# Windowed attention on one core: landing buffers for every load, GpSimd copies to fixed operand addresses, and another order of transfers

## The chip, the cores and the metric

One core of a Trainium2 chip runs the whole program; the other cores are idle. The metric is the device time of one execution in microseconds. Each kernel is timed several times; one execution is also recorded by the hardware profiler (for the changed kernel and the experiments it is one of the timed ones). Engines: PE is TensorE, PEld its weight loads, DVE VectorE, ACT ScalarE, POOL GpSimd, SP SyncE.

## The reference

Softmax attention inside windows of 64 rows, with 4 x 4096 rows of 1536 float32 values in each of q, k, v:

```python
B, S, D = 4, 4096, 1536; W = 64; nw = S // W
logits = np.einsum('bnwd,bnud->bnwu', q_w, k_w) * D ** -0.5   # q_w: (B, nw, W, D)
attn = softmax(logits)                                        # over the last axis
out = np.einsum('bnwu,bnud->bnwd', attn, v_w)                 # float32
```

Each input is read once (302 MB in all), the output written once (101 MB).

## The kernel before

The 16,384 rows are cut into 32 blocks (called units in the code) of 512. In each, TensorE transposes q and k (float16 pairs seen as float32), multiplies them, and after the exponentials multiplies by v. Loads cast float32 to float16 and are issued by GpSimd, as are the stores. TensorE's program is a loop over blocks, so its operands have fixed addresses: `q16`, `k16`, `v16`. VectorE and ScalarE raise `m_q`, `m_k`, `m_v` when TensorE has read the operand for the last time; only then may GpSimd load the next one there. The first blocks and the last v go by way of other buffers (cut). The main loop of GpSimd:

```python
for u in range(1, N - 1):                  # N = 32
    gp.wait_ge(m_q, u + 1)
    load("q", u + 1, q16, d_q)
    # ... (u == 1: v of block 1 copied from its staging place)
    if u + 1 < N - 1:
        store(u - 1)
    gp.wait_ge(m_k, u + 1)
    load("k", u + 1, k16, d_k)
    if u + 1 == N - 1:
        load("v", u + 1, vs, d_vs)
        store(u - 1)
    # ... (u == 1: v of block 2 copied from vs)
    elif u + 1 < N - 1:
        gp.wait_ge(m_v, u + 1)
        load("v", u + 1, v16, d_v)
gp.wait_ge(m_q, N)
store(N - 2)
# ... the last block is stored in two halves, by GpSimd and by SyncE
```

Note the order of transfers, which turns out to matter: **q, store, k, v**.

Of the kernel before, what the change touches and what calls it, by code (L numbers as in the profile page):

```python
# [8 lines left out]
FP16 = mybir.dt.float16  # L9
FP32 = mybir.dt.float32  # L10

P = 128
# [5 lines left out]
def kernel(  # L18
# [4 lines left out]
    v: bass.AP,  # L23
    out: bass.AP,
):



# [2 lines left out]
    nc = tc.nc  # L31
    PE, DVE, ACT = (getattr(mybir.EngineType, e) for e in ("PE", "DVE", "Activation"))
    B, S, D = q.shape
    DC = D // (2 * P)
    NJ = D // 512
    SLOTS, R, H = 4, 2, 2
# [5 lines left out]
    def sb(name, shape, dtype):  # L42
        return ctx.enter_context(nc.sbuf_tensor(name, shape, dtype))
# [6 lines left out]
    def sem(name):  # L50
        sems.append(nc.alloc_semaphore(name))
        return sems[-1]
# [1 line left out]
    q16 = sb("q16", [P, SLOTS, D], FP16)  # L54
    k16 = sb("k16", [P, SLOTS, D], FP16)
    v16 = sb("v16", [P, SLOTS, D], FP16)
    vs = sb("vs", [P, SLOTS, D], FP16)
    xq = sb("xq", [P, DC, UR], FP32)
    xk = sb("xk", [P, DC, UR], FP32)
    NO = 3  # L60
# [8 lines left out]
    ops = [ps(f"o{j}", [P, 512]) for j in range(NJ)]  # L69
    sp = ps("sp", [P, 4])  # L70

    d_r0, d_r1, d_r2, d_q, d_k, d_v, d_vs, d_q1, d_k1, d_v1 = (
        sem(n) for n in ("d_r0", "d_r1", "d_r2", "d_q", "d_k", "d_v", "d_vs", "d_q1", "d_k1", "d_v1")
    )
    d_o = [sem(f"d_o{i}") for i in range(NO)]
    d_l = [sem(f"d_l{i}") for i in range(2)]
    g_q, g_k, g_v = (sem(n) for n in ("g_q", "g_k", "g_v"))
# [8 lines left out]

    m_q, m_k, m_v = (sem(n) for n in ("m_q", "m_k", "m_v"))
    n_e = [sem("n_ed"), sem("n_ea")]
    i_d, i_p, c_q, done = sem("i_d"), sem("i_p"), sem("c_q"), sem("done")

    def on_act(n, j):
        return (n + j) % 2 == 0
# [3 lines left out]

    def slots(t, lo, hi, r):
        return t[:, lo:hi, :].rearrange("p (h r) d -> p h (r d)", r=r)

    def staged(i, half):  # L100

        return outs[i][:, 2 * half : 2 * half + 2, :].bitcast(FP16).rearrange(
            "p a (b d) -> p (a b) d", d=D
        )

    def load(name, u, dst, s):
        src = {"q": qf, "k": kf, "v": vf}[name]
        r = R if name == "v" else SLOTS
        nc.gpsimd.dma_start(  # L109
            out=slots(dst, 0, SLOTS, r), in_=rows(src, u * UR, SLOTS, r)  # L110
        ).then_inc(s, 16)
# [123 lines left out]
    def vector_unit(u):  # L235
        ve = nc.vector
        for g in range(0, 2 * DC, 2):
            copy_out(ve, ve.tensor_copy, g)
        if u == N - 1:
            ve.wait_ge(d_vs, 32)  # L240
            ve.wait_ge(m_v, N - 1)
            ve.tensor_copy(out=v16[:, :, :], in_=vs[:, :, :]).then_inc(g_v, 1)
        for n in range(H * R):
            if n % R == 0:
                await_(ve, p_s)
                ve.reciprocal(out=rs[:, n : n + R], in_=sp[:, n : n + R]).then_inc(n_d, 1)  # L246
                await_(ve, n_d)
                ve.sem_inc(n_r, 1)
            if n == 0:
                await_(ve, fr[0])  # L250
            for j in range(NJ):
                if not on_act(n, j):
                    await_(ve, p_o[0])
                    if (n, j) == (H * R - 1, NJ - 1):
                        ve.sem_inc(m_v, 1)  # L255
                    ins = ve.tensor_scalar_mul(  # L256
                        scaled(u, n, j), bank(n, j), scalar1=rs[:, n : n + 1]
                    )
                    told(ins, u, n, j, 0)
# [25 lines left out]
    def store(u):  # L285
        nc.gpsimd.dma_start(
            out=rows(of, u * UR, SLOTS, R), in_=slots(outs[u % NO], 0, SLOTS, R)
        ).then_inc(d_o[u % NO], 16)

    def unstage(src, dst, s):  # L290

        nc.gpsimd.tensor_copy(
            out=dst[:, :, :].bitcast(FP32), in_=src[:, :, :].bitcast(FP32)
        ).then_inc(s, 1)

    with tc.tile_critical(no_gpsimd_drain=True):

        raw = rows(qf, 0, SLOTS, SLOTS).rearrange("p h (r d) -> p (h r) d", d=D)
        for sl, s in ((slice(0, 1), d_r0), (slice(1, 2), d_r1), (slice(2, SLOTS), d_r2)):
            nc.sync.dma_start(out=outs[0][:, sl, :], in_=raw[:, sl, :]).then_inc(s, 16)  # L300
        nc.vector.memset(ident[:, :], 0.0).then_inc(i_d, 1)
        nc.gpsimd.wait_ge(i_d, 1)
        nc.gpsimd.wait_ge(d_r0, 16)
        nc.gpsimd.affine_select(
            out=ident[:, :], in_=ident[:, :], compare_op=mybir.AluOpType.not_equal,
            fill=1.0, base=0, pattern=[[-1, P]], channel_multiplier=1,
        ).then_inc(i_p, 1)
        load("k", 0, k16, d_k)
        load("v", 0, v16, d_v)

        for i in range(SLOTS):
            nc.gpsimd.wait_ge((d_r0, d_r1, d_r2, d_r2)[i], 16)
            nc.gpsimd.tensor_copy(out=q16[:, i, :], in_=outs[0][:, i, :]).then_inc(c_q, 1)
            if i == 1:
                load("q", 1, staged(2, 0), d_q1)
        load("k", 1, staged(2, 1), d_k1)
        load("v", 1, staged(1, 0), d_v1)
        load("v", 2, vs, d_vs)

        nc.vector.memset(ones[:, :], 1.0).then_inc(i_d, 1)  # L320
        nc.vector.memset(zeros[:, :], 0.0).then_inc(i_d, 1)
        for et in ets:
            nc.vector.memset(et[:, :, :, :], 0.0).then_inc(i_d, 1)
        nc.scalar.wait_ge(i_d, 5)
        nc.scalar.activation(zeros[:, 3:4], zeros[:, 0:1], EXP, bias=zeros[:, 0:1], scale=1.0)

        with nc.Fori(0, N, engines=OrderedEngineSet([PE]), head_slot={PE: 0}):
            tensor_unit()
        assert N % NO == 2
        for eng, unit in ((DVE, vector_unit), (ACT, scalar_unit)):  # L330
            with nc.Fori(0, N // NO, engines=OrderedEngineSet([eng]), head_slot={eng: 0}):
                for u in range(NO):
                    unit(u)
            for u in range(N - 2, N):
                unit(u)

        sy = nc.sync
        for j in range(NJ):
            for n in (2, 3):
                sy.sem_inc(f_o[j][n], 1)  # L340
        for a in range(2):
            sy.sem_inc(fr[a], NO)
        sy.wait_ge(i_p, 1)
        sy.wait_ge(i_d, 5)
        sy.wait_ge(c_q, SLOTS)
        sy.sem_inc(g_q, 1)
        for u in range(N):
            if u >= NO:
                sy.wait_ge(d_o[u % NO], 16 * (u // NO))
                for a in range(2):  # L350
                    sy.sem_inc(fr[a], 1)

            for d, g, n in (
                (d_q, g_q, u - 1 if u > 1 else 0),
                (d_k, g_k, max(u, 1) if u != 1 else 0),
                (d_v, g_v, 1 if u == 0 else u - 1 if 2 < u < N - 1 else 0),
            ):
                if n:
                    sy.sem_inc(g, 1)._wait_ge(d, 16 * n)

        gp = nc.gpsimd
        gp.wait_ge(d_q1, 16)
        gp.wait_ge(m_q, 1)
        unstage(staged(2, 0), q16, g_q)
        gp.wait_ge(d_k1, 16)
        gp.wait_ge(m_k, 1)
        unstage(staged(2, 1), k16, g_k)
        for u in range(1, N - 1):
            gp.wait_ge(m_q, u + 1)
            load("q", u + 1, q16, d_q)  # L370
            if u == 1:
                gp.wait_ge(d_v1, 16)
                gp.wait_ge(m_v, 1)
                unstage(staged(1, 0), v16, g_v)
            if u + 1 < N - 1:
                store(u - 1)
            gp.wait_ge(m_k, u + 1)
            load("k", u + 1, k16, d_k)
            if u + 1 == N - 1:
                load("v", u + 1, vs, d_vs)  # L380
                store(u - 1)
            if u == 1:
                gp.wait_ge(d_vs, 16)
                gp.wait_ge(m_v, 2)
                unstage(vs, v16, g_v)
            elif u + 1 < N - 1:
                gp.wait_ge(m_v, u + 1)
                load("v", u + 1, v16, d_v)
        gp.wait_ge(m_q, N)
        store(N - 2)  # L390


        base, o = (N - 1) * UR, outs[(N - 1) % NO]
        for h, (eng, c) in enumerate(((gp, 1), (sy, 3))):
            for a in range(2):
                eng.wait_ge(n_e[a], c)
            eng.dma_start(
                out=rows(of, base + R * P * h, R, R), in_=slots(o, R * h, R * h + R, R)
            ).then_inc(d_l[h], 16)
        gp.drain()  # L400
        for i in range(NO):
            last = max(u for u in range(N - 1) if u % NO == i)
            sy.wait_ge(d_o[i], 16 * (last // NO + 1))
        for i in range(2):
            sy.wait_ge(d_l[i], 16)
        sy.sem_inc(done, 1)
        gp.wait_ge(done, 1)
        lo, hi = min(s.num for s in sems), max(s.num for s in sems)
        assert hi - lo + 1 == len(sems)
        gp.sem_clear(range(lo, hi + 1))  # L410
# [30 lines left out]
```

## Time and profile before

| | before |
|---|---|
| median of the first 3 runs | 951.55 us (950.38 to 953.58) |
| profiled span | 949.5 us |
| HBM bytes | 402.65 MB, 424 GB/s over the span |
| PE, ACT, POOL busy | 64%, 35%, 10% |

The DMA side is full almost everywhere and no engine is; the prediction below shows the lines and reads them.

### The profile page before, as it was taken

How to read it: one execution, taken by the hardware profiler on the slowest of the kernel's cores; microseconds unless marked ns; L12 is line 12 of the kernel's file. 1: busy time of each engine (PE TensorE's matmuls, PEld its weight loads, DVE VectorE, ACT ScalarE, POOL GpSimd, SP SyncE). 2: the span in 40 equal slices, each digit the busy share in tenths (PEclk: the TensorE clock that was granted, in tenths of full speed). 3: DMA queues.
4: the chain of work that ended last, by engine and by line, in shares of the span. 5: the costliest groups of instructions: out<-in, count | busy, mean ns of one | idle time of the engine just before them, and what ended most of it. 6: DMA issues, size and time to landing. Idle time of an engine off the chain costs nothing. (4 is left out here: it accounts for less than half of the span.)

```text
span 949.5 us, 11240 instructions
## 1 busy us (share of the span) xinstructions
PE 609.7 (64%) x4096; PEld 393.6 (41%) x3456; DVE 278.7 (29%) x454; ACT 331.3 (35%) x642; POOL 97.4 (10%) x140
## 2 busy tenths in 40 slices
PE   2776855577565776656865558655577565776682
PEld 2544543354433444424544335443344433444450
DVE  1331413332133331333322333223332132331341
ACT  1442513443233432234432344323443233432252
POOL 4230100110001100101001010010110001100010
PEclk9997977997788987889887898787997788987796
DMA  9999999999999999999999999999999999999997
GB/s 249 216 284 283 238 247 282 279 284 267 235 277 281 285 280 238 261 280 283 283 254 245 281 280 284 272 234 272 281 283 281 243 256 281 282 282 261 235 236 300
DMA packets 26938, 253.34 MB, mean 267 GB/s; under 512 B 2096, under 2 KB 2096, under 8 KB 10544
## 3 DMA queue, kind: packets, MB, share of 16 engines
q0 software_dynamic: 26352, 248.52, 99.8%
q1 hardware_dynamic: 576, 4.72, 1.3%
q14 instruction: 8, 0.07, 0.0%
q8 instruction: 2, 0.03, 0.0%
HBM read 301.99 MB, written 100.66 MB: 424 GB/s over the span
## 5 line engine op out<-in xcount | busy, mean ns | idle before, releaser
L148 PE MATMUL tp<-ident,k 128*128 128x128 f32 x768 | 155.1, 349 | 231.4 <-PEq L214 224.9
L148 PEld LDWEIGHTS tp<-ident,k 128*128 128x128 f32 x768 | 120.4, 182 | 252.1 <-issue 249.6
L160 PE MATMUL lt<-xq,xk 128*128 128x256 f16 x1536 | 216.1, 293 | 0.0
L223 ACT COPY xk<-tp 128x512 f32<-128x512 f32 x96 | 59.2, 617 | 417.8 <-ACTq L214 417.8
L223 DVE COPY xk<-tp 128x512 f32<-128x512 f32 x96 | 66.5, 692 | 381.8 <-DVEq L214 381.8
L160 PEld LDWEIGHTS lt<-xq,xk 128*128 128x128 f16 x1536 | 160.1, 104 | 33.2
L148 PE MATMUL tp<-ident,q 128*128 128x128 f32 x768 | 104.0, 280 | 66.6 <-DVE xq L223 47.1
L148 PEld LDWEIGHTS tp<-ident,q 128*128 128x128 f32 x768 | 86.4, 143 | 100.5 <-issue 99.9
L269 ACT ACTIVATE et<-lt,zeros 32x128 f16<-32x128 f32 x256 | 92.0, 360 | 39.4 <-ACTq L214 36.2
L223 ACT COPY xq<-tp 128x512 f32<-128x512 f32 x96 | 59.3, 617 | 107.3 <-ACTq L214 107.3
L116 PE MATMUL o<-v,et 128*128 128x512 f16 x384 | 93.3, 379 | 0.0
L189 PEld LDWEIGHTS <-et 128*128 128x128 f16 x384 | 30.2, 97 | 151.3 <-issue 114.3
L256 DVE TENSOR_SCALAR out<-o,rs 128x512 f32<-128x512 f32 x128 | 90.2, 747 | 7.7
L223 DVE COPY xq<-tp 128x512 f32<-128x512 f32 x96 | 66.1, 689 | 78.0 <-DVEq L214 78.0
L116 PE MATMUL tp<-v,et 128*128 128x512 f16 x256 | 75.8, 377 | 0.0
L109 POOL DMA_DIRECT2D k<-in_k_dram x31 | 17.4, 562 | 416.5 <-ACTq L221 416.3
L246 DVE RECIPROCAL rs<-sp 128x2 f32<-128x2 f32 x64 | 10.6, 166 | 157.8 <-DVEq L214 157.6
L280 ACT ACTIVATE out<-tp,rs 128x512 f32<-128x512 f32 x64 | 44.0, 688 | 35.8 <-ACTq L214 31.3
L256 DVE TENSOR_SCALAR out<-tp,rs 128x512 f32<-128x512 f32 x64 | 48.1, 751 | 26.2 <-DVEq L214 26.2
L116 PE MATMUL lt<-v,et 128*128 128x512 f16 x128 | 48.3, 377 | 0.0
L109 POOL DMA_DIRECT2D v<-in_v_dram x29 | 20.5, 706 | 238.2 <-DVEq L255 238.2
L280 ACT ACTIVATE out<-o,rs 128x512 f32<-128x512 f32 x64 | 44.1, 688 | 0.0
(26 smaller groups left out, 132.6 us busy)
## 6 DMA issues: line engine op xcount, KB each, us to landing
out_dram<-out POOLq DMA_DIRECT2D x31, 3072.0 KB, 28.5
k<-in_k_dram POOLq DMA_DIRECT2D x31, 1536.0 KB, 20.6
q<-in_q_dram POOLq DMA_DIRECT2D x30, 1536.0 KB, 21.6
v<-in_v_dram POOLq DMA_DIRECT2D x29, 1536.0 KB, 18.9
vs<-in_v_dram POOLq DMA_DIRECT2D x2, 1536.0 KB, 29.7
out<-in_q_dram SPq DMA_DIRECT2D x2, 768.0 KB, 6.5
out<-in_q_dram SPq DMA_DIRECT2D x1, 1536.0 KB, 11.5
out<-in_q_dram POOLq DMA_DIRECT2D x1, 1536.0 KB, 22.7
```

Of the source, the lines that this page charges most:

```text
L109: nc.gpsimd.dma_start(out=slots(dst, 0, SLOTS, r), in_=rows(src, u * UR, SLOTS, r)).then_inc(s, 16)
L116: return nc.tensor.add_instruction(mybir.InstMatmult(name=nc.get_next_instruction_name(), engine=PE, ins=[low(rhs), low(w)], outs=[low(o)] ...
L148: ins = nc.tensor.transpose(tps[g % 2][:, r, j, :], pairs[:, c * P : (c + 1) * P], ident[:, :])
L160: ins = nc.tensor.matmul(lts[h][:, r, :, :], lhsT=halves(xk, c)[:, r, h, :, w], rhs=halves(xq, c)[:, :, h, :, w], start=(c == 0 and w == 0 ...
L189: ld = nc.tensor.ldweights(w)
L223: copy(out=dst, in_=tps[g % 2][:, :, :, :]).then_inc(f_c[g % 4], 1)
L246: ve.reciprocal(out=rs[:, n : n + R], in_=sp[:, n : n + R]).then_inc(n_d, 1)
L256: ins = ve.tensor_scalar_mul(scaled(u, n, j), bank(n, j), scalar1=rs[:, n : n + 1])
L269: ins = sc.activation(ets[h][s, :, :, s], lts[h][s, :, :, s], EXP, bias=zeros[s, 0:1], scale=scale)
L280: ins = sc.activation(scaled(u, n, j), bank(n, j), COPY, bias=0.0, scale=rs[:, n : n + 1])
```

## The change

The intent: GpSimd issues the next load as soon as it has copied a landed one away, instead of when TensorE has consumed it, so that transfers are queued well ahead; and at the end the last loads go ahead of stores that nobody waits for. The core of the diff (first blocks, SyncE's part and the removed VectorE copy of the last v are cut):

```diff
-    vs = sb("vs", [P, SLOTS, D], FP16)
+    ql = sb("ql", [P, SLOTS, D], FP16)
+    kl = sb("kl", [P, SLOTS, D], FP16)
+    NV = 2
+    vls = [sb(f"vl{i}", [P, SLOTS, D], FP16) for i in range(NV)]
...
+    def hand_over(src, dst, d, u, m, g):
+        gp = nc.gpsimd
+        gp.wait_ge(d, 16 * u)
+        gp.wait_ge(m, copies[0] // 3 + 1)
+        gp.tensor_copy(
             out=dst[:, :, :].bitcast(FP32), in_=src[:, :, :].bitcast(FP32)
-        ).then_inc(s, 1)
+        ).then_inc(c_l, 1)
+        copies[0] += 1
+        gp.wait_ge(c_l, copies[0])
+        gp.sem_inc(g, 1)
...
+        for u in range(1, N):
+            hand_over(ql, q16, d_q, u, m_q, g_q)
+            if u + 1 < N:
+                load("q", u + 1, ql, d_q)
+            hand_over(kl, k16, d_k, u, m_k, g_k)
+            if u + 1 < N:
+                load("k", u + 1, kl, d_k)
+            for what in {N - 3: "", N - 2: "-v"}.get(u, "s"):
+                if what == "v":
+                    load("v", N - 1, vls[(N - 1) % NV], d_v[(N - 1) % NV])
+                else:
+                    gp.wait_ge(m_q, u + 1)
+                    store(u - 2 if what == "-" else u - 1)
+            if u == N - 2:
+                store(u - 1)
+            hand_over(vls[u % NV], v16, d_v[u % NV], (u + u % NV) // NV, m_v, g_v)
+            if u + NV < N - 1:
+                load("v", u + NV, vls[u % NV], d_v[u % NV])
```

One thing that the few words about the change don't say: the store now follows the load of k. The order is **q, k, store, v**.

> **What bounds the kernel now.** I read the engine shares first, then the DMA row and the queues, then the waits, then windows of the start and the end. On the page:
>
> ```profile
> span 949.5 us, 11240 instructions
> PE 609.7 (64%) x4096; PEld 393.6 (41%) x3456; DVE 278.7 (29%) x454; ACT 331.3 (35%) x642; POOL 97.4 (10%) x140
> DMA  9999999999999999999999999999999999999997
> q0 software_dynamic: 26352, 248.52, 99.8%
> HBM read 301.99 MB, written 100.66 MB: 424 GB/s over the span
> ```
>
> No compute engine is near full; the DMA row is full in every slice but the last. The queue's byte count (253 MB) is smaller than the HBM traffic (402.65 MB) because a load reads float32 and lands float16. So in every GB/s figure of the profile a loading stretch shows half of what HBM gives.
>
> The waits of the kernel before, longest first for TensorE, and the sync engine's own:
>
> ```profile
> PE tp L148 <- PEq L214: 244.1, 33, 16.7
> PE tp L148 <- DVE xq L223: 47.9, 64, 1.0
> SPq L359 <- DMA k<-in_k_dram: 436.9, 31, 15.3
> SPq L359 <- DMA q<-in_q_dram: 243.5, 30, 36.4
> ```
>
> TensorE stands 244 us in 33 places, about one per block of 512 rows (32 blocks). SyncE, which passes on the landings of k, waits on the DMA of k. So TensorE starves for k some 7.5 us in each block. It looks like missing prefetch, but one asks first whether the DMA could have brought k sooner. The load of q for block 5 is issued at 121.48 us and that for block 31 at 886.21 us: (886.21 - 121.48) / 26 = 29.41 us a block. A block moves 3 loads and 1 store of 3.146 MB on the HBM side each, 12.58 MB: 427.9 GB/s, or 7.35 us a transfer. Now the stretches by window (columns: window and length; busy us of PE, PEld, DVE, ACT, POOL; TensorE clock, DMA share, GB/s):
>
> ```profile
> 0.00:40.00 40.00, 20.81 (x136) 13.70 (x116) 10.06 (x20) 12.50 (x23) 12.77 (x16) 1.00 0.97 236
> 100.00:880.00 780.00, 510.76 (x3432) 330.23 (x2893) 229.46 (x373) 275.07 (x535) 67.64 (x107) 0.85 1.02 270
> 880.00:900.00 20.00, 10.54 (x60) 7.87 (x56) 5.53 (x8) 4.91 (x8) 1.26 (x2) 0.74 1.03 225
> 900.00:909.00 9.00, 8.24 (x66) 4.85 (x52) 2.33 (x5) 5.23 (x13) 1.95 (x3) 1.00 0.84 160
> 909.00:943.00 34.00, 19.45 (x140) 10.92 (x111) 13.33 (x21) 12.32 (x24) 1.28 (x2) 0.87 0.99 341
> 943.00:949.50 6.50, 0.00 (x0) 0.00 (x0) 0.00 (x0) 0.00 (x0) 0.00 (x0) 0.50 0.02 9
> ```
>
> From 100 to 880 us the share is 1.02, that is, full. Windows of 3 us near the end with loads alone show 213 to 218 GB/s landed (426 to 436 read), and with stores alone 416 to 438. So loads, stores and the mean of a block all run at one rate, near 428 GB/s. It is a bound of bytes, not of latency. There is just **one hole**, at 900 to 909 us (0.84), and a quiet end of some 7 us after the last data, in which the last completion comes and the program closes.
>
> **What the Trainium skill says.** "DMA: Bandwidth & Descriptors", section Specifications, gives a fabric ceiling of 435 GB/s and an HBM limit of about 358 GB/s a core. The trace's 427.9 is 98% of the first and above the second, so here the first is the one to hold against, and at most 2% of rate is left. The same page, "Issuing engines are not separate DMA queues", says that all issuers share the same 16 engines: more buffers or earlier issues add no rate. The flat 428 GB/s over loads and stores agrees. "SBUF — State Buffer", section "SBUF: two separate sides", says that compute and DMA use separate ports, but that GpSimd and some two-port VectorE instructions lock each other out, and that a blocked GpSimd can't write descriptors. The trace before has GpSimd copies beside other work: during the copy at 34.55 to 37.29 us VectorE's multiply took 0.75 us, its mean over the run, and the DMA in 36 to 39 us landed 217 GB/s, full rate for loads. So no cost of such locks is seen. "GPSIMD Engine Reference", "Elementwise — side-by-side cycle accounting", has a port-bound body of 1.03 cycles an element: 3072 x 1.03 / 1.2 GHz = 2.64 us, an estimate; the trace has 2.75 us, which I use.
>
> **The change, part by part.**
>
> *Copies added.* Four such copies become 93 (31 blocks x q, k, v), so 89 more: 89 x 2.75 = 245 us of GpSimd. The cost of a copy and of an issue:
>
> ```profile
> L292 POOL COPY k<-out 128x3072 f32<-128x3072 f32 x1 | 2.8, 2752 | 4.5 <-DMA out<-in_k_dram 4.5
> L109 POOL DMA_DIRECT2D k<-in_k_dram x31 | 17.4, 562 | 416.5 <-ACTq L221 416.3
> L109 POOL DMA_DIRECT2D v<-in_v_dram x29 | 20.5, 706 | 238.2 <-DVEq L255 238.2
> ```
>
> A block then costs GpSimd 3 x 2.75 + 2 x 0.56 + 2 x 0.71 = 10.8 us of 29.4: no bound. POOL busy should come to about 97 + 245 = 342 us (36%). On the path of one operand a copy adds about 3 us after landing, with its semaphores.
>
> *Loads earlier.* The load of q is now issued when its landing buffer is copied out, not when TensorE has consumed the fixed one. Walk one block, with T = landing of q: q is copied and the next q issued at about T+4; k lands at T+7.35, is copied and reissued by T+12; the store follows, then the copy and reissue of v by T+17. Behind T the queue still holds k, store and v, 22 us of work. So at every issue 10 to 20 us are queued: never empty. But in the kernel before it wasn't empty either, from 100 to 880 us, so this is worth **0 us there**. TensorE needs about 16.9 us from the start of k to the end of a block (864.20 to 881.1) and 5 for q: 22 of 29.4, so it goes on waiting some 7 us, mostly for q instead of k (k is ready only some 7 us after q, so a short wait of 1 to 3 us stays there).
>
> *End.* In the kernel before, q of the last block is issued at 886.21, k not until 902.65, because it waits for TensorE to release k16, and the store that used to lie between them is held back. The queue runs dry at about 901. Now the loads of q and k of the last two blocks follow on the copies, with landings queued ahead of them; stores 28, 29 and 30 come after. The order of the queue becomes q30 k30 q31 k31 s28 v31 s29 s30 s31, each issued before the one ahead is finished by my walk. Hole by share: 9 x (1 - 0.84/1.02) = 1.6 us; by bytes against 215 GB/s: 9 x (1 - 160/215) = 2.3 us. I take **-2.0 us**.
>
> *What the end can give back.* Without the hole the DMA ends at about 942.5 - 2.0 = 940.5, its last transfer (s31) from 933.2. Backwards, 7.35 us each: s30 from 925.8, s29 918.5, v31 911.1, s28 903.8, k31 896.4, q31 889.1. So k30 lands at 889.1, is handed over by 894, TensorE ends block 30 at 911 and block 31 some 20.5 us later, at 931.5: its first half-store goes at about 932, ahead of 933.2. It fits by only 1 us, so I add **+0.3 us** for a slip. The VectorE copy of the last v (1.76 us, 923.8 to 925.6) goes away; TensorE was waiting for the exponentials until 926.2, and stores filled the queue: 0 us.
>
> Sum: 951.55 - 2.0 + 0.3 = 949.85, say **949.8 us**.
>
> **Rivals.** (1) *Prefetch frees TensorE*: the 244 us of waits shrink and the time with them. For it: the large wait. Against it: the DMA share of 1.02 at 98% of the stated ceiling; 402.65 MB at 435 GB/s are 925.6 us, an estimate with the skill's figure, and with 2 us of start and 7 of end 935, a gain of 1.7% at the very most. (2) *GpSimd becomes the bound or starves the queue*: it issues in order, so a wait for m_q ahead of a store holds up v behind it, and a copy delays an issue by 2.75 us. With 10 us queued at the worst it is hidden; were 1 us a block lost after all, it would be +31 us, 982. (3) *The end gets worse*: the last v waits for a copy and the three held stores bunch up; if TensorE finished block 31 some 4 us late, the last store would be alone, +3 us, 953. (4) *The transfers run at another rate*, because more of them are queued or GpSimd uses SBUF at the same time; 0.3% either way is 3 us. The start (loads alone, four queued, GpSimd copying) ran at full rate, so I give it little.
>
> **Range and chances.** The runs of the kernel before spread over 3.2 us themselves; the end can give or take 2 to 3, the rate 2 to 3. Range **946 to 954**. A gain over 2% needs below 932.5, under what (1) leaves at the ceiling: **0.01**. A loss over 2% needs case (2): **0.03**. Within 2%: **0.96**.
>
> **What would show it.** DMA share about 1.02 from 100 us to the end, the dip at 900 to 909 gone; about 29.4 us a block; POOL busy near 340 us; copies at 2.75 us; TensorE's waits for operands still near 240 us in total, now mostly before q; last data near 940 us. The prediction is wrong if the share sinks in the middle, if copies take much over 2.75 us or VectorE's rows grow, or if a block falls clearly below 29.4 us, which would mean that the rate wasn't a ceiling.

## The result, and the profile after

The changed kernel took **947.72 us** (946.70 to 948.15, 4 runs), the kernel before on the same chip 951.33 us (4 runs). The ratio is 0.9957 (95% interval 0.9938 to 0.9977): within 2%, and a real gain of some 4 us. Ratios here are the mean time of one kernel's fast runs over that of the other's of the same rounds, so not quite the ratio of the medians quoted. All runs of all kernels below were in the fast state.

The page of the changed kernel, its head lines:

```profile
span 946.4 us, 11421 instructions
PE 651.0 (69%) x4096; PEld 419.8 (44%) x3456; DVE 279.7 (30%) x453; ACT 332.8 (35%) x642; POOL 341.5 (36%) x229
DMA  9999999999999999999999999999999999999997
q0 software_dynamic: 26352, 248.52, 100.0%
HBM read 301.99 MB, written 100.66 MB: 425 GB/s over the span
```

POOL went from 97.4 to 341.5 us busy, and nothing on the DMA rows shows a difference. The copies in the groups of the page (columns: line, engine, operation, tiles, shape, count; busy us, mean ns; idle before and what ended it), then the waits of TensorE and GpSimd (total us, times, longest):

```profile
L292 POOL COPY q<-ql 128x3072 f32<-128x3072 f32 x31 | 85.0, 2743 | 395.7 <-DMA ql<-in_q_dram 395.5
L292 POOL COPY k<-kl 128x3072 f32<-128x3072 f32 x31 | 85.3, 2751 | 110.5 <-DMA kl<-in_k_dram 110.5
```

```profile
POOL q L292 <- DMA ql<-in_q_dram: 395.5, 30, 16.5
PE tp L147 <- PEq L213: 227.2, 60, 16.4
```

A copy takes 2.74 to 2.75 us, as foretold. TensorE waits about as long as before (227 against 244 us), now in 60 places instead of 33, mostly for q; and GpSimd itself waits 396 us for q to land. So everybody waits for the DMA, as before. Now the windows (columns as in the prediction):

```profile
100.00:880.00 780.00, 551.63 (x3440) 355.88 (x2900) 234.11 (x376) 278.75 (x539) 285.70 (x185) 0.84 1.02 270
880.00:900.00 20.00, 12.55 (x88) 10.59 (x89) 4.16 (x6) 3.77 (x6) 13.39 (x9) 0.83 0.98 193
900.00:909.00 9.00, 7.77 (x51) 2.55 (x28) 4.88 (x9) 6.95 (x15) 3.43 (x2) 1.00 0.99 326
```

The hole at 900 to 909 us is gone (share 0.99, before 0.84), but the 20 us ahead of it now are at 0.98 and 193 GB/s, where the kernel before had 1.03 and 225: there is a new, shallower hole. And a block takes (881.80 - 121.85) / 26 = 29.23 us, from the starts of the copies of q for blocks 4 and 30, against the 29.41 us of the prediction. The two are not measured alike: 29.41 us is taken between issues that wait for TensorE, and between the landings of q for the same blocks the kernel before takes 29.31 us (table below). Even so the gain may have come from where I had put 0 us, the middle.

**A view that the page doesn't print.** Every transfer raises its semaphore 16 times; the Trainium skill ("DMA: Bandwidth & Descriptors", "Why a DMA increments its semaphore by 16 and not by 1") says that the 16 engines finish independently and that each posts one of them. The trace keeps the time of each increment, and its numbers agree: 16 increments for every transfer, over 1.2 us and more in these two traces. The first increment tells how far the fastest engine is, the last one when the data may be used. I worked out from these records, for the 17th, 57th and 121st transfer (about blocks 4, 14 and 30) and for the very last increment (us from the span's start; "spread" is last minus first; these transfers are loads of q in the kernel before and of v in the changed one, and their neighbours of the other kinds show nearly the same spread):

| | 17th: first / last | 57th: first / last | 121st: first / last | spread at the 121st | last of all |
|---|---|---|---|---|---|
| before | 114.27 / 116.44 | 405.92 / 408.48 | 872.56 / 878.46 | 5.90 | 946.09 |
| changed | 112.98 / 114.52 | 404.93 / 407.83 | 871.57 / 874.47 | 2.90 | 942.87 |

In the kernel before **one of the 16 engines falls behind**: at the 121st transfer 15 engines are done within 2.56 us of the first and the last one comes at 5.90 us. From the 57th to the 121st transfer, 16 blocks, the spread grows from 2.56 to 5.90 us, 0.21 us a block. In the changed kernel it stays at 2.90. So over these 16 blocks the fastest engine takes 29.17 us a block in both kernels, and the slowest 29.37 us before and 29.17 us now. The fastest engines gain 1.3 us by block 4 and nothing more (1.0 us at block 30). That gain is another thing than the lag: in the kernel before, the 16th and 17th transfer come 8.11 and 7.61 us after the one ahead by first increments, where some 7.3 is usual, probably because v was issued only at 96.34 us, 2.2 us before the fastest engine was done with what was queued (98.55); no run tests that by itself. By the last increment, which is what anybody waits for, the changed kernel is 4.0 us ahead at the 121st transfer and 3.2 us ahead at the end. So the end, where the prediction had put the whole gain, gave 0.8 us back.

### The profile page after: what moved, and what is told of

It reads as the page before. It is cut to its first block, busy times and chain, and to the rows that moved or that the text cites. A ratio compares the mean times of both kernels' runs of the same rounds, so it can differ in the third digit from the quotient of the medians.

```text
span 946.4 us, 11421 instructions
## 1 busy us (share of the span) xinstructions
PE 651.0 (69%) x4096; PEld 419.8 (44%) x3456; DVE 279.7 (30%) x453; ACT 332.8 (35%) x642; POOL 341.5 (36%) x229
## 5 line engine op out<-in xcount | busy, mean ns | idle before, releaser
L147 PE MATMUL tp<-ident,q 128*128 128x128 f32 x768 | 165.0, 384 | 185.6 <-PEq L213 172.7
L147 PEld LDWEIGHTS tp<-ident,q 128*128 128x128 f32 x768 | 131.2, 200 | 239.4 <-issue 236.8
L292 POOL COPY q<-ql 128x3072 f32<-128x3072 f32 x31 | 85.0, 2743 | 395.7 <-DMA ql<-in_q_dram 395.5
L159 PE MATMUL lt<-xq,xk 128*128 128x256 f16 x1536 | 210.2, 288 | 0.0
L147 PE MATMUL tp<-ident,k 128*128 128x128 f32 x768 | 136.3, 317 | 67.3 <-PEq L213 54.5
L159 PEld LDWEIGHTS lt<-xq,xk 128*128 128x128 f16 x1536 | 156.8, 102 | 30.4
L147 PEld LDWEIGHTS tp<-ident,k 128*128 128x128 f32 x768 | 105.1, 163 | 86.3 <-issue 83.9
L292 POOL COPY k<-kl 128x3072 f32<-128x3072 f32 x31 | 85.3, 2751 | 110.5 <-DMA kl<-in_k_dram 110.5
L292 POOL COPY v<-vl 128x3072 f32<-128x3072 f32 x31 | 85.5, 2758 | 10.4 <-DMA vl<-in_v_dram 10.4
```

Of the source, the lines that this page charges most:

```text
L147: ins = nc.tensor.transpose(tps[g % 2][:, r, j, :], pairs[:, c * P : (c + 1) * P], ident[:, :])
L159: ins = nc.tensor.matmul(lts[h][:, r, :, :], lhsT=halves(xk, c)[:, r, h, :, w], rhs=halves(xq, c)[:, :, h, :, w], start=(c == 0 and w == 0 ...
L292: gp.tensor_copy(out=dst[:, :, :].bitcast(FP32), in_=src[:, :, :].bitcast(FP32)).then_inc(c_l, 1)
```

## The experiments

Two theories were on record. **E** (the prediction's): the gain is the filled hole of the end. **L** (laggard): the gain is the lagging engine, whatever makes it lag. Twelve runs were made in three sessions, each session on one chip and beside the kernel before (medians 952.23, 951.58 and 952.24 us). Experiments 1, 2, 3 and the plain end of 8 are of the first session, 4, 5 and 7 of the second, the rest of the third. All gave correct results but the two pure streams, which are wrong on purpose.

### 1. The changed kernel once more

No edit.

> The changed kernel once more, as a control on this chip. Both theories: ratio 0.996 to the kernel before (about -3.5 us). Theory E (the end: the gain is the filled hole at 900 us) expects nothing of the middle. Theory L (laggard: one of the 16 DMA engines falls behind in the kernel before by some 0.18 us a block, its completion comes 5.9 us after the first at block 30, and only some 0.06 us a block, 2.9 us, in the changed one) expects the spread of the 16 completions to be about 3 us again at block 30; if it is anything else here the laggard is chance.

Measured: 948.3 us, ratio 0.9952 (0.9929 to 0.9975); spread 3.38 us at the 121st transfer. The result holds in another session, and the small spread isn't chance.

### 2. The kernel before with its hole filled

```diff
-            if u + 1 < N - 1:
-                store(u - 1)
+            store(u - 1)
             gp.wait_ge(m_k, u + 1)
             load("k", u + 1, k16, d_k)
             if u + 1 == N - 1:
                 load("v", u + 1, vs, d_vs)
-                store(u - 1)
```

> The kernel before, with store 29 in its usual place ahead of the last load of k, so that the queue has 7.3 us of work while that load waits for TensorE. Theory E: the hole at 900 to 909 us goes and with it 1.6 to 2.3 us (about 949.3). Theory L: the laggard was never idle in that hole (its completions go on every 7.28 us through it), so the dip goes from the DMA share but the time moves by less than 0.7 us.

Measured: 952.29 us, ratio 0.9994 (0.9977 to 1.0011), spread 6.45. The hole is gone and the time isn't less. The windows of this experiment from 900 us on, in two answers of the same view, tell why:

```profile
900.00:909.00 9.00, 8.25 (x66) 4.50 (x49) 2.73 (x5) 5.37 (x12) 1.27 (x2) 1.00 0.99 369
930.00:951.40 21.40, 10.10 (x73) 4.70 (x51) 6.92 (x10) 7.23 (x15) 0.55 (x1) 0.80 0.42 175
```

The dip moved: share 0.99 at 900 us, but 0.42 after 930 us, with TensorE still 10 us busy there. The kernel before has 0.64 from 930 us to its end, with TensorE nearly done:

```profile
930.00:949.50 19.50, 1.75 (x9) 0.20 (x2) 2.43 (x5) 1.84 (x3) 0.57 (x1) 0.60 0.64 272
```

The store put ahead of k delays the last k (landed 922.87 us, before 915.11), so the last block is computed late; its first half-store is issued at 941.03 instead of 931.89 us, when the stores ahead of it are already done (937.84). So this run doesn't refute that the hole cost something; it shows that filling it with a store is no gain, since the last block then comes late. By its time it can't decide between E and L. The increments of the kernel before say more: from q to k of the last block the first increment takes 10.35 us (901.71 to 912.07), the last one 7.28 (907.83 to 915.11). In that hole the fast engines stood idle and the slowest did not, as L had it.

### 3. The kernel before with the other order, and nothing else

```diff
-            if u + 1 < N - 1:
-                store(u - 1)
             gp.wait_ge(m_k, u + 1)
             load("k", u + 1, k16, d_k)
+            if u + 1 < N - 1:
+                store(u - 1)
```

> The kernel before, with each store issued after the load of k instead of before it, the order of transfers (q, k, store, v) that the changed kernel has; no copies, no landing buffers. If the order is what makes the laggard: spread at block 30 falls from 5.9 to about 3 us and the time by 2 to 3 us. If it is the copies or buffers: spread stays near 6 us and the time within 1 us of before.

Measured: **945.9 us**, ratio 0.9930 (0.9911 to 0.9947), spread 3.36. Two moved lines, without a buffer or a copy, gain more than the whole change, and twice what was expected. It ran once more in the third session:

> The kernel before with stores after the load of k, once more, beside the others of this chip: ratio to the kernel before 0.993, about 945.5, if the first result holds; spread about 3.4 us at block 30.

Measured: 945.23 us, ratio 0.9928 (0.9911 to 0.9944), spread 2.98. In the trace of the first of these two runs, the gain on the kernel before by last increments is 1.9 us at the 17th transfer, 3.7 us at the 121st and 5.1 us at the end. Its middle by windows, under that of the kernel before in the prediction, shows that the DMA share can't tell the two apart:

```profile
100.00:880.00 780.00, 556.55 (x3400) 333.49 (x2858) 232.60 (x374) 278.93 (x537) 66.69 (x107) 0.84 1.02 268
```

1.02 here and 1.02 there: a mean over 16 engines says full whether or not one of them lags.

### 4. The changed kernel with the old order

```diff
             if u + 1 < N:
                 load("q", u + 1, ql, d_q)
+            if u < N - 3:
+                gp.wait_ge(m_q, u + 1)
+                store(u - 1)
             hand_over(kl, k16, d_k, u, m_k, g_k)
```

(and the store after the load of k taken out for those blocks)

> The changed kernel with each store (except at its end) issued ahead of the copy of k, so that the order of transfers is q, store, k, v as in the kernel before. Order as cause: spread grows to about 6 us at block 30 and the time by 2 to 3 us, to about 950. Copies or buffers as cause: within 0.7 us of the changed kernel.

Measured: 951.56 us, ratio 1.0002 (0.9983 to 1.0022), spread 5.83. With the order undone, the buffers, the copies and the new end together gain nothing.

### 5. The order of transfers without any compute

The same loads and stores, two buffers each, no TensorE, VectorE or ScalarE work but a memset, no copies; two kernels that differ in the order alone.

> Wrong result on purpose: the same loads and stores, order q, k, store, v, two buffers each, no compute and no GpSimd copies; stores write zeros. The floor of the transfers: 402.65 MB at 428 to 431 GB/s are 934 to 941 us and with start and end about 942 to 949 us. If it comes to 945 or more, the changed kernel is at the floor; if under 940, compute or GpSimd still costs. Theory L with the copies as cause: spread at block 30 like or above the kernel before, near 6 us. With the order as cause: near 3 us or less.

> The same stream in the order q, store, k, v of the kernel before. If the order makes the laggard: spread at block 30 some 3 us more than in the stream of the other order and 2 to 3 us slower. If not: the two streams agree within 0.7 us.

Measured: 948.71 us (ratio 0.9968, 0.9951 to 0.9985) for q, k, store, v; 949.57 us (0.9972, 0.9951 to 0.9993) for q, store, k, v. Spreads at the 121st transfer 3.40 and 5.33, with one engine last in the old order (the 15th increment comes 1.46 us after the first). So the old order has a lagging engine even here, but not the expected 2 to 3 us of time: 0.9 us between the medians, and the intervals overlap. The four runs of the old order fall into two pairs, about 948.4 and 950.7 us, and the one profiled is of the longer pair; whether the lag is there in the shorter one isn't known. And it grows slowly: from the 57th to the 121st transfer the spread gains 0.98 us (0.52 in the new order), with compute 3.3 and more. These streams are no floor either: by bytes they are 1.2 us behind experiment 3 at the start (first increment of their 15th transfer at 114.23 and 114.28 us, of its 17th at 113.00; q of block 0 is one transfer here and three there), they issue the last stores only when the last v has landed (934.38 us in the new order), and kernels with compute beat them.

### 6. What follows the store

```diff
             if u + NV < N - 1:
                 load("v", u + NV, vls[u % NV], d_v[u % NV])
+            if u < N - 3:
+                gp.wait_ge(m_q, u + 1)
+                store(u - 1)
```

(and the store after the load of k taken out for those blocks: order q, k, v, store)

> The changed kernel with each store (but for its end) after the load of v, in the order q, k, v, store, q. It asks what makes the lagging engine: in the order q, store, k, v the store is followed by a load of 12,288-byte packets (k); in q, k, store, v by one of 6,144-byte packets (v). Here it is followed by q, of 12,288-byte packets. If the packets of the next load matter: spread of completions at block 30 near 6 us and about 951. If what matters is that k comes right after q, without a store between them, or anything else: spread near 3 us and 947 to 949.

Measured: 949.95 us, ratio 0.9980 (0.9959 to 1.0001), spread 4.81. With the same end, the new order had 0.9952 and a spread of 3.38 (experiment 1), the old one 1.0002 and 5.83 (experiment 4): this is between them in time, though its interval overlaps both. The spread of 4.81 isn't the lag of the old order: it was 4.51 at the 57th transfer already and grew by 0.30 us since, and five engines, not one, are over 3.3 us behind the first. From the 57th to the 121st transfer the three kernels with compute in the order q, store, k, v grow by 3.34, 3.57 and 3.50 us; all seven with compute in the order q, k, store, v by 0.00 to 0.28. So here, too, no engine keeps falling behind. The packet records were the next thing to look at. A store consists of packets of 12,288 bytes that mostly take 0.46 us. I counted those between 450 and 850 us that took over 0.488 us:

| order, kernel | over 0.488 us | spread at the 121st |
|---|---|---|
| q, store, k, v: before / experiment 2 / 4 | 31 / 29 / 47 | 5.90 / 6.45 / 5.83 |
| q, k, v, store: experiment 6 | 32 | 4.81 |
| q, k, store, v: changed / 1 / 3 / 3 again | 9 / 7 / 5 / 0 | 2.90 / 3.38 / 3.36 / 2.98 |
| the two streams (new / old order) | 0 / 0 | 3.40 / 5.33 |

Where the store is followed by a load of k or q (packets of 12,288 bytes) there are some 30 long packets or more; where v follows (packets of 6,144 bytes) under 10. But the stream in the old order lags without any, and experiment 6 has 32 without a growing lag. Nor are they long enough: in the kernel before the 31 packets exceed 0.46 us by 1.1 us in all, while the spread grew by some 2.9 in these 400 us (an estimate, at 0.21 us a block). So what makes the engine lag is **not settled**: the order decides it, that is shown; by what mechanism, and why one engine, is not. The trace here doesn't number the engines. The Trainium skill ("DMA: Bandwidth & Descriptors", "Latency and other measured facts") says that two of them, 7 and 15, are usually slower and guesses at the fetching of descriptors for GpSimd's transfers; here one engine lags and only in one order, which that alone doesn't explain, and no run shows the cause.

### 7. The cost of the copies

Every copy done twice:

```diff
-        gp.tensor_copy(...).then_inc(c_l, 1)
-        copies[0] += 1
+        for _ in range(2):
+            gp.tensor_copy(...).then_inc(c_l, 1)
+            copies[0] += 1
+            gp.wait_ge(c_l, copies[0])
```

> The changed kernel with every GpSimd copy done twice: POOL busy about 341 + 256 = 597 us. If the copies are hidden behind queued transfers, as predicted, the middle stays at 29.2 us a block and the time grows by under 1 us there, plus up to 3 us at the end where the queue runs low. If GpSimd delays issues on the path: 2.75 us times some of 31 blocks, tens of us.

Measured: 950.15 us, ratio 0.9983 (0.9961 to 1.0005), spread 2.28. From its page, then from its windows:

```profile
PE 657.1 (69%) x4096; PEld 420.7 (44%) x3456; DVE 279.7 (29%) x453; ACT 333.5 (35%) x642; POOL 596.7 (63%) x322
```

```profile
100.00:880.00 780.00, 554.59 (x3446) 356.94 (x2909) 233.09 (x375) 278.14 (x537) 505.24 (x265) 0.84 1.02 270
```

255 us more of GpSimd cost the middle nothing: the 121st transfer is done at 873.73 us, against 874.47 in the changed kernel. The 2 to 3 us that the time grew lie after it, at the end, where the queue is shallow. So the copies are hidden, as predicted.

### 8. The end by itself

The changed kernel with plain stores, each after the load of k, to the end:

```diff
-            for what in {N - 3: "", N - 2: "-v"}.get(u, "s"):
-                ... (as in the diff above)
-            if u == N - 2:
-                store(u - 1)
+            gp.wait_ge(m_q, u + 1)
+            store(u - 1)
```

(and v of the last block loaded as every other)

> The changed kernel without its order of the end: every store right after the load of k, the last v loaded in its usual place. Theory E, as predicted, holds that the reordered end is what gains: without it, 1.5 to 2 us slower than the changed kernel. Rival: the reordered end makes its own dips (share 0.87 at 885 to 888 and under 1 at 894 to 900 us), so without it the dips go and the time is the same or up to 1.5 us faster than the changed kernel (946 to 948).

Measured: 950.54 us, ratio 0.9981 (0.9965 to 0.9998), against 0.9952 of the changed kernel in the same session: by these ratios 2.8 us slower, by medians 2.2 (the intervals overlap a little). So against a plain end the reordered one seems to gain, as E says: with plain stores, store 30 is done at 932.90 us and the first half-store of the last block is issued only at 937.23. The kernel before, however, didn't have a plain end; it had its own early loads. So the changed kernel with the end of the kernel before:

```diff
+            if u == N - 2:
+                load("v", N - 1, vls[(N - 1) % NV], d_v[(N - 1) % NV])
+            gp.wait_ge(m_q, u + 1)
+            store(u - 1)
```

(in place of the same lines)

> The changed kernel with the end of the kernel before: store 28 in its usual place after the load of k, then q31, k31, v31, store 29, store 30. The kernel before in the other order (b_ksv) was 2.4 us faster than the changed kernel on one chip, and both had the same 29.2 us a block and the same time at block 30. If the difference is the changed end, whose held-back stores let the queue run low at 885 to 900 us: about 946, 2 to 3 us faster than the changed kernel. If it is the copies: no gain, 948 or more.

Measured: **944.5 us**, ratio 0.9919 (0.9902 to 0.9935), spread 2.64: the fastest kernel of all, and 3.4 us (0.0036 of 951) better than the changed one by ratios to the kernel before, though of different sessions. What its end has over the changed one is seen in the windows of 3 us. The changed kernel:

```profile
885.00:888.00 3.00, 2.87 (x13) 2.46 (x14) 0.69 (x1) 0.62 (x1) 0.53 (x1) 0.50 0.87 156
...
894.00:897.00 3.00, 3.00 (x29) 2.73 (x28) 0.69 (x1) 0.63 (x1) 3.00 (x3) 1.00 0.95 152
897.00:900.00 3.00, 3.00 (x29) 2.62 (x28) 0.69 (x1) 0.63 (x1) 2.77 (x2) 1.00 0.93 187
```

and this experiment:

```profile
885.00:888.00 3.00, 2.87 (x13) 2.45 (x13) 0.69 (x1) 0.62 (x1) 0.56 (x1) 0.50 0.97 291
...
894.00:897.00 3.00, 3.00 (x20) 2.50 (x21) 0.69 (x1) 0.60 (x2) 3.00 (x2) 0.69 1.04 250
897.00:900.00 3.00, 3.00 (x29) 2.70 (x27) 0.69 (x1) 0.86 (x2) 0.06 (x1) 1.00 1.03 220
```

Loads alone land some 215 GB/s when the queue is full; the changed kernel shows 156, 152 and 187 there. GpSimd's timeline in the changed kernel (start us, length us, operation, idle before) has the cause:

```profile
881.80 2.75 POOL L292 COPY q<-ql 128x3072 f32<-128x3072 f32 x1 [15.18 <-DMA ql<-in_q_dram]
885.13 0.53 POOL L108 DMA_DIRECT2D ql<-in_q_dram  x1 [0.58 <-POOL q L292]
889.07 2.75 POOL L292 COPY k<-kl 128x3072 f32<-128x3072 f32 x1 [3.41 <-DMA kl<-in_k_dram]
892.41 0.53 POOL L108 DMA_DIRECT2D kl<-in_k_dram  x1 [0.58 <-POOL k L292]
892.93 0.71 POOL L281 DMA_DIRECT2D out_dram<-out  x1
```

At 885.13 only the k of block 30 is still under way, and its first engine is done at 886.08: the store that used to be queued behind it is held back. The new q is issued 0.95 us ahead of that, and its first completion comes 8.52 us after the one before instead of 7.3; the following k takes 9.98 us by last increments. Leaving store 28 at its place fills exactly this gap.

Not all of the 3.4 us is this gap as such. In the two traces store 30 is done 3.3 us earlier with the old end (933.17 against 936.47), the last increment only 1.2 us earlier (941.63 against 942.87); the other 2.2 us lie between it and the end of the program, 1.3 against 3.5 us. In all kernels with compute the program ends either about 1.3 us after the last increment of SyncE's half of the last store or about 3.5 us (3.4 to 3.6) after that of GpSimd's, whichever is later; in this experiment it is SyncE's, in the kernel before and the changed one GpSimd's. Whether that follows from the gap isn't tested.

### 9. Stores from SyncE

The changed kernel with a plain end, and its stores 0 to 30 issued by SyncE on a queue of its own.

> The changed kernel with the stores issued by SyncE, on its own queue, so that they share the engines with the loads instead of waiting behind them; GpSimd issues loads alone. By bytes the time stays within 3 us of the changed kernel (loads and stores all run at one rate). If the laggard comes from stores in GpSimd's queue, the spread falls under 2.5 us and the time by 1 to 2 us; if the mixing of two queues costs rate, it is slower.

Measured: 962.55 us, ratio 1.0109 (1.0092 to 1.0126), spread 4.54. The main expectation, a time within 3 us, failed; its last branch, slower, came: against the plain end of experiment 8 (0.9981) it is 1.3% slower. The 121st transfer is done at 881.17 us instead of 873.91, so the loss is there in the middle, with a DMA share of 1.02 again; the mean store packet takes 0.4715 us instead of 0.4611. Stores from SyncE cost rate here. Whether it is the second queue, the place of the stores among the loads or SyncE's own waits (it issues a store and waits for another in turn) isn't separated.

## Why the prediction was right or wrong

The time fell in the range, on the right side and within 2%. The sum came near for reasons that were half wrong: -1.7 us was foretold and some -4 measured, and that it is not further off is luck, since two errors of about 7 and 5 us (the order, the end) were of opposite sign.

- **The bound: right.** Bytes at 16 engines' rate. (Loads alone landed 205 to 227 GB/s in those windows, not 213 to 218; their mean is the 215 that was used.) All kernels with GpSimd stores lie within 1% of each other; doubling GpSimd's work or putting TensorE's waits elsewhere moved nothing in the middle. Rival 1 was dismissed rightly.
- **The copies: right.** 2.75 us each, POOL 341.5 us against 342 predicted, hidden. With the old end they cost nothing measurable (0.9919 with, 0.9928 without, same session).
- **"So this is worth 0 us there": wrong, and the largest error.** I had written the new order of the queue down without noticing that the place of the store in it was a change, and read the mean share of 1.02 as "nothing to gain". Order alone is worth 0.70 to 0.72%, 6.7 to 6.9 us of 952 (experiment 3). By last increments 1.9 us of it come by block 4, about as much again by block 30, and the rest at the end. Of the 1.9 us some 1.1, by first increments, are the late transfers near 100 us, so "just one hole" was wrong too. From block 4 on it is the engine that no longer lags; in my terms rival 4, "another rate", which I had given little. Even the "quiet end of some 7 us after the last data" hid it: six packets of GpSimd's half-store run one after another from 942.88 to 945.63 us, when all others are done.
- **The end, -2.0 us + 0.3 us: wrong in sign.** The hole at 900 went, but my walk of the queue, "each issued before the one ahead is finished", was too loose at one place. It compared the issue of q31 with the last landing of k30, not with the first engine's completion, and left out the time from issue to data; the margin was then 0.95 us and a new gap opened at 885 us. Against the end of the kernel before, the new end costs about 3.4 us (experiment 8). And the -2.0 us was a mean over engines: the slowest one, for which each completion waits, was never idle in the old hole (experiment 2).
- **The sum** by ratios: order -0.72%, copies and buffers -0.09%, end +0.38% give the -0.43% measured, but this is the same runs read backwards and checks nothing. The check is experiment 4, which has the copies and the new end without the order: +0.29% would follow, +0.02% (-0.17 to +0.22) was measured. So the parts don't quite add, and some 2 us are not accounted for. The close of the program may be among them: experiment 8's end has 1.3 us after the last increment, and the kernel before, the changed one and experiment 4 have 3.1 to 3.5.
- **What would show it**: copies, POOL and TensorE's waits came as said; the "about 29.4 us a block" came as 29.23, against 29.31 before when measured alike. I had named a block below 29.4 us as the sign that the rate was no ceiling, and so it was: the 29.4 us were not the rate of the 16 engines, whose fastest took 29.17 us before and after, but that of the slowest.

## What to carry to other kernels

A DMA share of 1 says that the engines are busy on average, not that the slowest of them, which each completion waits for, is as fast as the rest: compare the first and last of the 16 increments over the run. Where the queue bounds a kernel, try the order of loads and stores in it before buying buffers and copies; here two moved lines gained 6.7 us, and the whole change, which had the same order, more buffers and a worse end, about 4. And at the end of a stream, hold no transfer back unless what remains queued covers the time from the next issue to its first byte, counted from the fastest engine (0.95 us did not, in experiment 8).

## What the Trainium skill lacked or had wrong

- "DMA: Bandwidth & Descriptors" doesn't have it that the order of loads and stores in one queue changes how far one engine lags: from the 57th to the 121st transfer the spread grows by 3.3 to 3.6 us in the kernels with compute in the order q, store, k, v, and by 0.3 or less in those in the order q, k, store, v; for the kernel before that order is worth 0.7% of the time (945.9 against 952.23 us).
- The same page says that spreading transfers over issuing engines doesn't help bandwidth. It doesn't have that it can hurt: with the stores on SyncE's queue this kernel was 1.3% slower than with all on GpSimd's (ratios 1.0109 and 0.9981).
- Its table of specifications lists an HBM limit of about 358 GB/s a core; with the other cores idle the kernel before moved 427.9 GB/s in its middle. The page says elsewhere that such figures depend on the other core; in the table only the bracket (a stack over two cores) hints at it.
- No page describes comparing the first and the last of the 16 increments over a run to see a lagging engine where a trace doesn't number the engines: a DMA share of 1.02 stood for kernels with a spread of 5.90 us and of 3.36 us alike.
